# State-space phase of a two-layer encoder: input scaling, phase products and given states on VectorE, copied operands in a PSUM bank of their own

## Chip, cores, metric

One core of a Trainium2 chip runs the whole program. The metric is the device time of one execution in microseconds (us). Engines are named as in the profile: PE (TensorE matrix products, with PEld for its weight loads), DVE (VectorE), ACT (ScalarE), POOL (GpSimd), SP (SyncE, which issues most DMAs).

## The reference, cut to what matters

The program is one inference step of a two-layer encoder on 512 new positions of a prompt stream and 32 of a running stream, 1024 wide, in float32. Layer 0 mixes tokens with a complex diagonal state-space model (S5), layer 1 with retention; each is followed by cross-attention to memory tokens and a convolutional feed-forward part. The change lies in the S5 mixer alone:

```python
def s5_block(state, u, a_bar, b_bar, c):
    bu = jnp.einsum('gpc,blgc->blgp', b_bar, u.astype(jnp.complex64))
    bu = bu.at[:, 0].add(a_bar * state)
    a = jnp.broadcast_to(a_bar, bu.shape)
    _, xs = lax.associative_scan(_linear_combine, (a, bu), axis=1)
    y = jnp.real(jnp.einsum('gcp,blgp->blgc', c, xs))
    return xs[:, -1], y
```

There are 64 groups of 16 channels with 64 complex states each. `u` is the input after an RMS norm, so each position is scaled by one over its root mean square. The running stream starts from a given complex state, the prompt from zero. Beside the S5 mixer, both layers need keys and values of 256 memory tokens: four products of 256 x 1024 by 1024 x 1024, which do not depend on the stream.

## The kernel before, in words

**First phase, `phase1`.** It holds the S5 mixer of layer 0 up to its GELU, and, as filling, the memory keys and values of both layers. The 1024 channels go in eight tiles e = 0..7 of eight groups each. Time is cut in chunks of 8 positions, which gives 64 chunks for the prompt and 4 for the running stream, laid side by side in 70 columns (`POS`). The recurrence over chunks is turned into a real one: the states are multiplied by unit phases `ph` (parts `pr`, `pi`: 32 columns of states by 70 chunks), a real scan with the decay `rho8` runs along the chunks, and the result is turned back by the same phases.

The steps for one tile are functions of their own:

- `powers(e)` (V): scales the tile's input `u` by `ur`, one over the root mean square (L826, 128x560), and makes products of decay powers and input matrices: four on DVE (L834, L835), two sums on POOL (L836).
- `phases()` (P): once, makes `ph` by doubling. The squarings (L770 to L779) give columns 1, 2, 4, .., 64; five doublings fill the columns between by six complex products of 32, 96, 224, 480, 480 and 512 elements per partition. Each complex product is `cmul` (L580 to L589): six operations, of which the two second products (L585, L588) go to the engine `eng2`, here POOL, and four stay on DVE (L584, L586, L587, L589).
- `matrices(e)` (M): PE transposes (L848), ACT copies (L849, L855), PE products (L853, L856), a sum on DVE (L860) whose operand comes from POOL (L858), and eight small DMAs (L863).
- `states(e)` (S): PE products (L876) put the chunk inputs of a tile, real and imaginary, in two PSUM banks `v[0]`, `v[1]`. ACT copies a loaded operand `ca` (L880, two copies of 128x128) into free columns of the same two banks, and for five tiles also the input matrices of tile e+2 (`bbe`, L884, two copies of 128x64). DVE multiplies by the phases in place (L893 to L897). ACT then writes the given states into chunk column 65 of both banks (L898, L899).
- `carry(e)` (C): six products and sums on DVE from `ca` (L938 to L942).
- `scan(e)` (Z): on DVE, two scans (L915), the products back (L916, L917) and the sums (L921, L922); ACT copies the last states out (L924, L925).
- `outputs(e)` (O): PE products (L953, L954), GELU on ACT (L955), PE transposes (L963), ACT copies (L965, L966).

**Order.** The program text issues `PROLOGUE`: V0, P, M0, V1, S0, C0, Z0, M1, V2, and then for each e S(e+1), C(e+1), V(e+3), Z(e+1), O(e), M(e+2). At points marked F it puts in units of the memory keys and values: 16 units for layer 0 (plain products, L528) and 16 for layer 1 (weights split in two parts, products L240 to L242). A layer-1 unit's weights are loaded, cast and negated on ACT (L229, L230), and completed by an adding DMA issued from POOL (L235). Within the data's dependences each engine's queue is ordered by the framework's scheduler from a timeline that it estimates when the program is built; on the chip every engine goes through its queue in that order. An instruction that waits therefore holds up all that is behind it on its engine.

**Buffers.** The eight PSUM banks of this phase are one pool (`bank`). A tile taken from it is one whole bank and is free again after its last reader. The framework orders all accesses of different engines to one such tile, whichever columns they touch.

**After `phase1`** follow the GLU (`glu`, its weights split in L208 and L209 as everywhere after), attention, feed-forward, retention, and the second layer's attention and feed-forward, made of dense products on PE (L249).

Of the kernel before, what the change touches and what calls it, by code (L numbers as in the profile page):

```python
# [13 lines left out]
OP = mybir.AluOpType  # L14
# [3 lines left out]
P = 128  # L18
# [14 lines left out]
C = 16  # L33
NP = 32
L = 8
POS = 70
# [136 lines left out]
class Kernel:  # L173
# [417 lines left out]
    def phase1(self, sp):  # L591
        nc, io = self.nc, self.io
        V, A, PL = nc.vector, nc.scalar, nc.gpsimd
# [14 lines left out]
        def st(shape, tag, bufs=1, dt=F32):  # L608
            return sp.tile(shape, dt, tag=tag, bufs=bufs, name=self.name(tag))

        def load(key, shape, src=None, bufs=1, eng=None):
            t = st(shape, key, bufs)
            (eng or nc.sync).dma_start(out=t, in_=io[key] if src is None else src)
            return t
# [15 lines left out]
        s0 = load("s0", [P, 64])  # L630
# [15 lines left out]
        def sm(tag, keep=False):  # L646

            if keep:
                return st([P, N], tag)
            if not short:  # L650
                a = self.slot(5 * N)
                short.extend(a[:, n * N:(n + 1) * N] for n in range(5))
            return short.pop()
# [25 lines left out]
        k, r, q = (sm(f"q{n}") for n in range(3))  # L679
# [21 lines left out]
        for s in (1, 2, 4):  # L701
            o = [a[:, :, s + 1:2 * s + 1] for a in (Pr, Pi)]
            a = [a[:, :, 1:s + 1] for a in (Pr, Pi)]
            b = [a[:, :, s:s + 1].to_broadcast([P, N, s]) for a in (Pr, Pi)]
# [23 lines left out]
        V.tensor_tensor(out=u2, in0=am1, in1=li, op=OP.mult)  # L728
        V.tensor_tensor(out=ci_, in0=ci_, in1=u2, op=OP.subtract)
        V.tensor_tensor(out=ci_, in0=ci_, in1=den, op=OP.mult)  # L730
        bb = [st([P, NP, C], n) for n in ("bbr", "bbi")]
        bt = [self.slot(512).rearrange("p (n c) -> p n c", c=C) for _ in range(2)]
        for n in range(2):
            PL.tensor_tensor(out=braw[n], in0=braw[n], in1=gp, op=OP.mult)
# [13 lines left out]
        um, ut, ur = st([P, POS], "um"), st([P, POS], "ut"), st([P, POS], "ur")  # L748
# [4 lines left out]
        s0n = st([P, NP], "s0n")  # L753
# [11 lines left out]
        pr, pi = ph[:, 0], ph[:, 1]  # L765
        w1, w2, wt = (st([P, 2, NP, 1], f"w{n}") for n in range(3))

        def square(o, a):

            V.tensor_tensor(out=wt, in0=a, in1=a, op=OP.mult)  # L770
            V.tensor_tensor(out=o[:, 0], in0=wt[:, 0], in1=wt[:, 1], op=OP.subtract)
            V.scalar_tensor_tensor(out=o[:, 1], in0=a[:, 0], scalar=2.0, in1=a[:, 1], op0=OP.mult, op1=OP.mult)

        def unit(c):

            V.tensor_tensor(out=wt, in0=c, in1=c, op=OP.mult)
            V.tensor_tensor(out=wt[:, 0], in0=wt[:, 0], in1=wt[:, 1], op=OP.add)
            V.tensor_scalar(out=wt[:, 0], in0=wt[:, 0], scalar1=-0.5, scalar2=1.5, op0=OP.mult, op1=OP.add)
            V.tensor_tensor(out=c, in0=c, in1=wt[:, 0:1].to_broadcast([P, 2, NP, 1]), op=OP.mult)  # L779

        def phases():
            V.tensor_tensor(out=rho8, in0=rho[:, :NP], in1=rho[:, :NP], op=OP.mult)
            V.tensor_tensor(out=rho8, in0=rho8, in1=rho8, op=OP.mult)
            V.tensor_tensor(out=rho8, in0=rho8, in1=rho8, op=OP.mult)
            PL.memset(pr[:, :, 0:1], 1.0)
            PL.memset(pi[:, :, 0:1], 0.0)
            square(w1, csn[:, :, :NP].unsqueeze(3))
            square(w2, w1)
            square(ph[:, :, :, 1:2], w2)
            unit(ph[:, :, :, 1:2])  # L790
            s = 2
            while s <= 64:
                n = min(s, POS - 5 - s)
                square(ph[:, :, :, s:s + 1], ph[:, :, :, s // 2:s // 2 + 1])
                unit(ph[:, :, :, s:s + 1])
                if n > 1:
                    step = 16 if n == 32 else n
                    for o in range(0, n, step):
                        lo = max(o, 1)
                        w = o + step - lo  # L800
                        t = [self.slot(512)[:, :NP * w].rearrange("p (n s) -> p n s", s=w) for _ in range(2)]
                        self.cmul(V, [a[:, :, s + lo:s + o + step] for a in (pr, pi)],
                                  [a[:, :, lo:o + step] for a in (pr, pi)],
                                  [a[:, :, s:s + 1].to_broadcast([P, NP, w]) for a in (pr, pi)], t, PL)
                s *= 2
            for a in (pr, pi):
                PL.tensor_copy(out=a[:, :, 65:70], in_=a[:, :, 0:5])
# [9 lines left out]
        bbe = {e: [b3[:, n, e] for n in range(2)] for e in range(3)}  # L817
        self.g32 = []

        def powers(e):  # L820

            d = E[e]
            p0 = 4 * e
            d["cbd"] = load("cbd", [P, 2, 4, 2 * C], io["cbd"][e].rearrange("p (r n c) -> p r n c", r=2, n=4), 3)
            u = d["u"] = U[e].rearrange("p (g q) -> p g q", g=8)
            PL.tensor_tensor(out=u, in0=u, in1=ur.unsqueeze(1).to_broadcast([P, 8, POS]), op=OP.mult)  # L826

            sh = [P, 4, L, C]
            bs = [a.unsqueeze(2).to_broadcast(sh) for a in bbe.pop(e, [b[:, p0:p0 + 4] for b in bb])]
            pw = [a[:, p0:p0 + 4, :L].unsqueeze(3).to_broadcast(sh) for a in (Pr, PRn, PIn)]  # L830
            vb, vt = [self.slot(512).rearrange("p (n j c) -> p n j c", n=4, j=L) for _ in range(2)], \
                [self.slot(512).rearrange("p (n j c) -> p n j c", n=4, j=L) for _ in range(2)]
            for n in range(2):
                V.tensor_tensor(out=vb[n], in0=pw[n], in1=bs[n], op=OP.mult)  # L834
                V.tensor_tensor(out=vt[n], in0=pw[2], in1=bs[1 - n], op=OP.mult)  # L835
                PL.tensor_tensor(out=vb[n], in0=vb[n], in1=vt[n], op=OP.add)  # L836
            d["vb"] = [[b[:, i].rearrange("p j c -> p (j c)") for i in range(4)] for b in vb]
# [27 lines left out]
        def states(e):  # L865


            d = E[e]
            p0, g0 = 4 * e, 8 * e
            u, Vt = d["u"], d["Vt"]  # L870
            ca = load("ca", [P, 2, 8, C], io["ca"][e].rearrange("p (r n c) -> p r n c", r=2, n=8), 2)
            banks = [self.bank() for _ in range(2)]
            d["v"] = v = [b[:, :280].rearrange("p (n q) -> p n q", n=4) for b in banks]
            for n in range(2):
                for i in range(8):
                    nc.tensor.matmul(v[n][(i % 2) * 64:(i % 2 + 1) * 64, i // 2], lhsT=Vt[n][:, i * 64:(i + 1) * 64], rhs=u[:, i],  # L876
                                     start=True, stop=True)
            d["ca"] = [b[:, 280:408].rearrange("p (n c) -> p n c", c=C) for b in banks]
            for n in range(2):
                A.copy(d["ca"][n], ca[:, n])  # L880
            if e and e + 2 < KT:
                bbe[e + 2] = [b[:, 408:472].rearrange("p (n c) -> p n c", c=C) for b in banks]
                for n in range(2):
                    A.copy(bbe[e + 2][n], bb[n][:, p0 + 8:p0 + 12])  # L884
            phs = [a[:, p0:p0 + 4] for a in (pr, pi)]
            pos3 = [P, 4, POS]

            d0 = d["d0"] = st(pos3, "d0")
            PL.tensor_tensor(out=d0, in0=posmask.unsqueeze(1).to_broadcast(pos3),
                             in1=rho8[:, p0:p0 + 4].unsqueeze(2).to_broadcast(pos3), op=OP.mult)  # L890
            x = d["x"] = pair()
            for n in range(2):
                V.tensor_tensor(out=x[n], in0=v[n], in1=phs[0], op=OP.mult)  # L893
                V.tensor_tensor(out=v[n], in0=v[n], in1=phs[1], op=OP.mult)

            V.tensor_tensor(out=v[1], in0=x[0], in1=v[1], op=OP.subtract)
            V.tensor_tensor(out=v[0], in0=x[1], in1=v[0], op=OP.add)  # L897
            A.copy(v[1][:, :, 65], s0[:, p0:p0 + 4])  # L898
            A.copy(v[0][:, :, 65], s0n[:, p0:p0 + 4])  # L899

        def pair():
            t = self.slot(SLOT)
            return [t[:, n * 280:(n + 1) * 280].rearrange("p (n q) -> p n q", n=4) for n in range(2)]
# [41 lines left out]
        def outputs(e):  # L945
# [21 lines left out]
            self.g32.append(g32)  # L967

        fn = dict(V=powers, S=states, Z=scan, C=carry, M=matrices, O=outputs, P=lambda e: phases())
        done = set()  # L970

# [455 lines left out]
```

## Time and profile before

| | |
|---|---|
| three runs | 1888.02, 1890.13, 1890.9 us; median 1890.13 |
| the profiled execution | 1889.96 us, of which 1888.1 us are the profile's span |
| PE busy in the span | 1821.8 us (96%) |
| DVE, ACT, POOL busy | 1036.9, 636.5, 293.1 us |
| first dense product of the GLU (L249) | 243.04 us after the span's start |
| mean granted PE clock, 0 to 50, 50 to 100, 100 to 150, 150 to 200, 200 to 250 us | 0.97, 0.86, 0.84, 0.90, 0.93 |
| the same, 250 to 450 us | 1.00 |

The span is the time between the first and the last recorded instruction; the time of an execution has 1.9 us more. Times in rows count from the span's start. A row of a timeline gives start, duration, engine, line, operation, the tile written and the tiles read, the count of merged instructions, and in brackets the engine's idle time before it with what ended it. Where instructions of one line are merged, the duration is that of the whole row. A row of waits gives the total, the number of times and the longest.

### The profile page before, as it was taken

The page shows a single profiled execution, that of the slowest core. Times are in us where ns is not written, and L with a number is a line of the kernel's source. Part 1 is how long each engine was busy: PE and PEld are TensorE (multiplying, and loading weights), DVE is VectorE, ACT ScalarE, POOL GpSimd, SP SyncE. Part 2 cuts the span into 40 slices and gives each one's busy share as a digit, 9 for nine tenths or more (in the row PEclk, how much of TensorE's full clock was granted, in tenths as well). Part 3 has the DMA queues.
Part 4 walks back from the last instruction along what each step waited for, and adds up shares of the span by engine and source line. Part 5 has one row for each costly group of instructions (what it writes and reads, how often), then busy time and mean ns, then how long its engine had stood idle before and what let it go on. Part 6 is the DMA issues. An engine that isn't in the chain of part 4 may idle for free.

```text
span 1888.1 us, 32839 instructions
## 1 busy us (share of the span) xinstructions
PE 1821.8 (96%) x13815; PEld 1732.8 (92%) x13815; DVE 1036.9 (55%) x1827; ACT 636.5 (34%) x977; POOL 293.1 (16%) x368
## 2 busy tenths in 40 slices
PE   8877899999999999999999999999999999999998
PEld 7466799999999999999899899998899999999997
DVE  7686756545534535555545645546654554453553
ACT  3244554443323313333223222233443332232333
POOL 2522101011201202220000100100101121120221
PEclk9979999999999999999999999999999999999998
DMA  6737743122222222222222222222321222222221
GB/s 240 205 93 188 184 137 115 68 86 84 85 90 90 83 97 88 80 92 84 73 96 85 78 87 68 91 78 89 133 68 58 89 88 83 88 84 95 90 71 67
DMA packets 68274, 186.41 MB, mean 99 GB/s; under 512 B 9184, under 2 KB 18784, under 8 KB 68128
## 3 DMA queue, kind: packets, MB, share of 16 engines
q1 hardware_dynamic: 65536, 175.79, 28.0%
q0 software_dynamic: 2304, 8.39, 2.5%
q8 instruction: 108, 1.77, 0.4%
q14 instruction: 38, 0.31, 0.1%
q10 hardware_dynamic: 288, 0.15, 0.0%
HBM read 171.16 MB, written 10.77 MB: 96 GB/s over the span
## 4 chain that ended last, share of the span: by engine, by line
PE 84%; DVE 2%; ACT 1%; issue 1%; DMA 0%; ACTq 0%; DVEq 0%
PE ps L249 75%; PE ps L240 2%; PE ps L241 2%; PE ps L242 2%; PE ps L1351 1%; DVE wl L209 1%; PE ps L1340 0%; PE ps L1313 0%; PE ps L1073 0%; ACT wh L208 0%; PE ps L1287 0%; DMA wl<-in_w_v 0%; PE bank L1087 0%; DVE xl L308 0%; PE ps L345 0%
## 5 line engine op out<-in xcount | busy, mean ns | idle before, releaser
L249 PE MATMUL ps<-xh,wh 128*128 128x272 f32 x2432 | 507.5, 290 | 5.4 <-DVE x L372 3.6
L208 ACT CAST wh<-wr 128x1024 fp32r<-128x1024 f32 (+1 forms) x240 | 247.7, 1036 | 760.1 <-PE ps L249 641.2
L249 PE MATMUL ps<-xl,wh 128*128 128x272 f32 x2432 | 503.6, 288 | 0.0
L249 PE MATMUL ps<-xh,wl 128*128 128x272 f32 x2432 | 502.3, 288 | 0.0
L249 PE MATMUL ps<-r,wh 128*128 128x272 f32 x2688 | 449.0, 289 | 3.0 <-ACT r L966 1.6
L249 PEld LDWEIGHTS ps<-xh,wh 128*128 128x128 f32 x2432 | 380.6, 188 | 11.2 <-ACT r L314 3.8
L249 PEld LDWEIGHTS ps<-r,wh 128*128 128x128 f32 x2688 | 379.9, 189 | 6.4 <-ACT r L208 3.0
L249 PEld LDWEIGHTS ps<-xh,wl 128*128 128x128 f32 x2432 | 382.0, 188 | 2.3 <-issue 2.3
L249 PEld LDWEIGHTS ps<-xl,wh 128*128 128x128 f32 x2432 | 383.0, 189 | 0.3
L209 DVE TENSOR_TENSOR wl<-wr,wh 128x1024 fp32r<-128x1024 f32 (+1 forms) x240 | 296.8, 1239 | 98.0 <-ACT wh L208 89.2
L249 PE MATMUL ps<-r,wl 128*128 128x272 f32 x1344 | 278.1, 288 | 0.0
L249 PEld LDWEIGHTS ps<-r,wl 128*128 128x128 f32 x1344 | 211.1, 189 | 0.0
L372 DVE TENSOR_TENSOR x<-ps,x 128x544 f32<-128x544 f32 x96 | 69.3, 724 | 235.1 <-PE ps L249 234.9
L317 POOL TENSOR_TENSOR acc<-acc,r 128x544 f32<-128x544 f32 x36 | 58.7, 1631 | 466.1 <-ACT r L314 457.7
L1160 DVE TENSOR_TENSOR r<-ps,rr 128x544 f32<-128x544 f32 x44 | 31.9, 725 | 96.6 <-PE ps L249 96.6
L1150 DVE TENSOR_TENSOR r<-ps,rr 128x272 f32<-128x272 f32 x44 | 19.4, 442 | 117.7 <-PE ps L249 117.7
L208 ACT CAST r<-r 128x544 fp32r<-128x544 f32 x84 | 52.5, 650 | 65.4 <-POOL r L1161 25.7
L1153 POOL COPY nco<-r 128x2 f32<-128x2 f32 x44 | 13.9, 316 | 374.5 <-DVE r L1151 374.5
L1158 DVE SCALAR_TENSOR_TENSOR r<-r,conv,r 128x546 f32<-128x546 f32 x88 | 69.1, 785 | 3.5 <-ACT r L1156 1.9
L1161 POOL TENSOR_TENSOR r<-r,r 128x32 f32<-128x32 f32 x44 | 35.2, 799 | 206.2 <-ACT wh L208 186.2
L209 DVE TENSOR_TENSOR r<-r,r 128x544 fp32r<-128x544 f32 x84 | 59.3, 728 | 12.8 <-ACT r L208 12.6
L1211 POOL TENSOR_TENSOR r<-r,r 128x544 f32<-128x544 f32 x8 | 10.9, 1357 | 339.9 <-ACT wh L208 325.9
(347 smaller groups left out, 2036.4 us busy)
## 6 DMA issues: line engine op xcount, KB each, us to landing
wr<-in_w_r SPq DMA_DIRECT2D x48, 512.0 KB, 3.2
wr<-in_w_a SPq DMA_DIRECT2D x44, 512.0 KB, 3.2
wr<-in_w_g SPq DMA_DIRECT2D x44, 512.0 KB, 3.3
wr<-in_w_d SPq DMA_DIRECT2D x32, 448.0 KB, 3.4
wr<-in_w_k SPq DMA_DIRECT2D x16, 512.0 KB, 5.1
wr<-in_w_v SPq DMA_DIRECT2D x16, 512.0 KB, 3.6
wr<-in_w_q SPq DMA_DIRECT2D x16, 512.0 KB, 3.7
wr<-in_w_o SPq DMA_DIRECT2D x16, 512.0 KB, 3.3
```

The source lines that it names most:

```text
L208: self.nc.scalar.copy(hi, src)
L209: (self.nc.gpsimd if pool else self.nc.vector).tensor_tensor(out=lo, in0=src, in1=hi.bitcast(F32), op=OP.subtract)
L240: mm(out, lhsT=a[0], rhs=b[0], start=start, stop=False)
L241: mm(out, lhsT=a[0], rhs=b[1], start=False, stop=False)
L242: mm(out, lhsT=a[1], rhs=b[0], start=False, stop=stop)
L249: mm(ps[:, h, :TH], lhsT=ws[wi], rhs=x[xi][:, h * TH:(h + 1) * TH], start=start and n == 0, stop=stop and n == 2)
L317: add.tensor_tensor(out=self.acc, in0=self.acc, in1=sq, op=OP.add)
L372: self.nc.vector.tensor_tensor(out=self.halves(x), in0=src, in1=self.halves(x), op=OP.add)
L1150: V.tensor_tensor(out=ext[:, 2:2 + TH], in0=pa[:, 0, :TH], in1=r[:, :TH], op=OP.mult)
L1158: V.scalar_tensor_tensor(out=cv, in0=ext[:, t:t + W], scalar=cw[:, t, f:f + 1], in1=cv, op0=OP.mult, op1=OP.add)
L1160: V.tensor_tensor(out=self.halves(gr), in0=pg[:, :, :TH], in1=self.halves(r), op=OP.mult)
L1161: PL.tensor_tensor(out=gr[:, TP:], in0=gr[:, TP:], in1=cv[:, TP + 2:W], op=OP.mult)
```

## The change

Five edits in `phase1`, no other function is touched:

1. The input scaling L826 goes from POOL to DVE (eight instructions).
2. The second products of the six complex products in `phases` (L585, L588, twelve instructions) go from POOL to DVE.
3. The two writes of given states per tile (L898, L899, sixteen instructions) go from ACT to DVE.
4. `ca` and `bbe` are copied into a third bank `cb` that `states` takes from the pool, in place of free columns of the banks of `v`.
5. With one target bank, the two copies of `ca` become one, and so do the two of `bbe` (for this the two parts of `bb` are put in one tile `bball`).

```diff
-        bb = [st([P, NP, C], n) for n in ("bbr", "bbi")]
+        bball = st([P, 2, NP, C], "bb")
+        bb = [bball[:, n] for n in range(2)]
...
-                                  [a[:, :, s:s + 1].to_broadcast([P, NP, w]) for a in (pr, pi)], t, PL)
+                                  [a[:, :, s:s + 1].to_broadcast([P, NP, w]) for a in (pr, pi)], t)
...
-            PL.tensor_tensor(out=u, in0=u, in1=ur.unsqueeze(1).to_broadcast([P, 8, POS]), op=OP.mult)
+            V.tensor_tensor(out=u, in0=u, in1=ur.unsqueeze(1).to_broadcast([P, 8, POS]), op=OP.mult)
...
-            d["ca"] = [b[:, 280:408].rearrange("p (n c) -> p n c", c=C) for b in banks]
-            for n in range(2):
-                A.copy(d["ca"][n], ca[:, n])
+            cb = self.bank()
+            d["ca"] = [cb[:, n * 128:(n + 1) * 128].rearrange("p (n c) -> p n c", c=C) for n in range(2)]
+            A.copy(cb[:, :256].rearrange("p (r n c) -> p r n c", r=2, n=8), ca)
             if e and e + 2 < KT:
-                bbe[e + 2] = [b[:, 408:472].rearrange("p (n c) -> p n c", c=C) for b in banks]
-                for n in range(2):
-                    A.copy(bbe[e + 2][n], bb[n][:, p0 + 8:p0 + 12])
+                b4 = cb[:, 256:384].rearrange("p (n i c) -> p n i c", n=2, c=C)
+                bbe[e + 2] = [b4[:, n] for n in range(2)]
+                A.copy(b4, bball[:, :, p0 + 8:p0 + 12])
...
-            A.copy(v[1][:, :, 65], s0[:, p0:p0 + 4])
-            A.copy(v[0][:, :, 65], s0n[:, p0:p0 + 4])
+            V.tensor_copy(out=v[1][:, :, 65], in_=s0[:, p0:p0 + 4])
+            V.tensor_copy(out=v[0][:, :, 65], in_=s0n[:, p0:p0 + 4])
```

## The prediction

> **What bounds the kernel now.** I read the page first, then the chain that ended last, then the busy times by stage, then waits and timelines of single engines.
>
> ```profile
> span 1888.1 us, 32839 instructions
> PE 84%; DVE 2%; ACT 1%; issue 1%; DMA 0%; ACTq 0%; DVEq 0%
> ...
> 243.04 58.57 PE ps L249 x455
> ...
> 46.00:82.50 36.50, 35.76 (x148) 19.26 (x146) 20.43 (x34) 8.40 (x13) 21.32 (x24) 1.00 0.69 202
> 82.50:101.60 19.10, 6.29 (x58) 4.47 (x57) 18.82 (x34) 6.11 (x17) 7.01 (x7) 0.58 0.75 218
> 101.60:113.40 11.80, 6.58 (x33) 5.96 (x33) 11.71 (x26) 4.87 (x12) 2.88 (x3) 0.64 0.13 34
> 113.40:180.50 67.10, 57.01 (x561) 50.77 (x561) 50.33 (x106) 32.55 (x76) 19.71 (x22) 0.93 0.59 144
> 180.50:243.00 62.50, 48.03 (x360) 39.60 (x358) 38.12 (x77) 30.52 (x70) 9.42 (x11) 0.92 0.68 169
> ```
>
> The chain is PE for 84% of the span, and from 243.04 us on it is dense products in long unbroken pieces. The change touches nothing behind that point, so its worth is the time by which 243.04 moves. The lower rows are the stretch before it: length, then busy time of PE, PEld, DVE, ACT and POOL, granted clock, DMA share, GB/s. Up to 82.5 us PE is full (35.76 of 36.50). Between 82.5 and 113.4 it is busy 12.87 of 30.9 us, at a clock of 0.58 and 0.64, while DVE is full. So 18.0 us of PE time lie open there; at full clock the 12.87 would be 6.29 x 0.58 + 6.58 x 0.64 = 7.9, another 5.0. After 113.4 PE is idle 10.1 us in 67.1 and 14.5 us in 62.5: a loop over tiles that neither engine fills.
>
> Why DVE is full but late is in the timelines of POOL and DVE.
>
> ```profile
> 57.94 9.89 POOL L826 TENSOR_TENSOR u<-u,ur 128x560 f32<-128x560 f32 x8 [31.80 <-issue]
> 67.79 0.26 POOL L585 TENSOR_TENSOR r<-ph 128x32 f32<-128x32 f32 x1
> ...
> 68.28 2.49 POOL L836 TENSOR_TENSOR r<-r,r 128x512 f32<-128x512 f32 x2
> ...
> 85.45 1.23 POOL L588 TENSOR_TENSOR r<-ph 128x512 f32<-128x512 f32 x1
> ...
> 45.87 0.28 DVE L779 TENSOR_TENSOR ph<-ph,w 128x64 f32<-128x64 f32 x1
> ...
> 54.49 0.45 DVE L746 TENSOR_REDUCE ssum<-bank 128x70 f32<-128x280 f32 x1 [5.72 <-PE bank L744]
> ...
> 59.52 0.68 DVE L835 TENSOR_TENSOR r<-PIn,bank 128x512 f32<-128x512 f32 x1
> 68.08 0.30 DVE L586 TENSOR_TENSOR ph<-ph,r 128x32 f32<-128x32 f32 x1 [7.89 <-POOL r L585]
> ...
> 76.91 5.30 DVE L587 TENSOR_TENSOR ph<-ph 128x480 f32<-128x480 f32 x1
> ...
> 91.92 0.79 DVE L893 TENSOR_TENSOR r<-bank,ph 128x280 f32<-128x280 f32 x2
> ```
>
> POOL waits 31.8 us for the scale `ur`, then scales all eight inputs in a row (9.89 us); the first second product of the phases stands behind them at 67.79, although its inputs were there at 46.15 (L779, the last squaring step, ends then). DVE waits 7.89 us for it, goes on at POOL's pace, and reaches the first tile's L893 only at 91.92. The sums of V0 on POOL (L836), which PE's first transposes need, stand behind the scalings too.
>
> ```profile
> PE bank L848 <- POOL r L836: 7.2, 2, 6.7
> PE bank L876 <- ACT xl L849: 5.2, 3, 2.0
> PE bank L954 <- DVE r L922: 3.9, 2, 2.3
> PE bank L953 <- DVE r L921: 3.6, 1, 3.6
> PE bank L848 <- DVE xl L942: 2.0, 3, 0.8
> ...
> PE bank L241 <- DMA wl<-in_w_v: 6.6, 2, 5.1
> ```
>
> These are PE's waits between 46 and 243 us. The longest of the first four (6.7, 2.0, 2.3, 3.6) lie in the open stretch and together are 14.6 us: all four end with work that stands behind the phases on DVE, or behind POOL's backlog.
>
> **The change, part by part.** The durations for what moves to DVE:
>
> ```profile
> 36.08 0.22 DVE L584 TENSOR_TENSOR ph<-ph 128x32 f32<-128x32 f32 x1
> ...
> 71.86 0.39 DVE L589 TENSOR_TENSOR ph<-ph,r 128x96 f32<-128x96 f32 x1
> 72.16 0.38 DVE L584 TENSOR_TENSOR ph<-ph 128x224 f32<-128x224 f32 x1
> ...
> 74.89 0.66 DVE L584 TENSOR_TENSOR ph<-ph 128x480 f32<-128x480 f32 x1
> ...
> 83.26 0.68 DVE L584 TENSOR_TENSOR ph<-ph 128x512 f32<-128x512 f32 x1
> ...
> L372 DVE TENSOR_TENSOR x<-ps,x 128x544 f32<-128x544 f32 x96 | 69.3, 724 | 235.1 <-PE ps L249 234.9
> ...
> L898 ACT COPY bank<-s x8: 156/165/165, 94.3 to 226.4; 128x4 f32<-128x4 f32 x8
> ```
>
> *Phases (edit 2).* One operation of each of the six complex products costs 0.22 + 0.39 + 0.38 + 0.66 + 0.66 + 0.68 = 3.0 us together. The twelve moved ones are 6.0 us on DVE; all 36 are 18.0 us, and need nothing from another engine any more. Their inputs are complete at 46.15, and DVE's 5.72 us of idle time before L746 can take a part, so 12.3 us are left behind the scale. How many go there depends on the scheduler's estimate: the bounds are none and all.
>
> *Scaling (edit 1).* 724 ns for 544 elements gives 0.745 us for 560, eight times 6.0 us on DVE, against 9.89 on POOL. What goes: POOL is free for the sums of V0 as soon as L835 is done, at 60.2 instead of 68.28. On the path are the first scaling, which S0 needs, and at most the second; the other six fall behind or into DVE's waits (DVE is idle 16.8 us between 113.4 and 180.5), at no cost unless DVE becomes the pace.
>
> *The first L893.* V0 ends on DVE at 59.52 + 0.68 = 60.2. Add one scaling (0.75) and the 12.3 us of phases: 73.2. With V1 in between (four products of 0.68 and a scaling, 3.5) it is 76.7. So it comes 15 to 19 us earlier. If no idle time is used and V1 and all scalings go first: 60.2 + 6.0 + 18.0 + 2.7 = 86.9, 5 us earlier. If DVE is no limit at all, PE is: 18.0 + 5.0 = 23 us. PE is the nearer bound, because it has to do the layer-0 keys and values in any order. I take its four longest waits, 14.6, and half of what the clock can give, 2.5: 17 us. What is late next is PE itself.
>
> *The own bank (edits 4, 5).* One tile of the loop, and one exception:
>
> ```profile
> L893 DVE TENSOR_TENSOR r<-bank,ph 128x280 f32<-128x280 f32 x16 | 7.0, 441 | 9.2 <-ACT bank L884 8.8 <-ACT bank L880 0.4
> ...
> 137.36 0.21 ACT L924 COPY stout<-r 128x8 f32<-128x8 f32 x1 [4.68 <-DVE r L921]
> ...
> 141.47 1.19 PE L876 MATMUL bank<-u,xl 128*64 128x70 f32 x32
> ...
> 143.79 0.20 ACT L884 COPY bank<-bbr 128x64 f32<-128x64 f32 x1
> ...
> 144.03 0.45 DVE L893 TENSOR_TENSOR r<-bank,ph 128x280 f32<-128x280 f32 x1 [2.02 <-ACT bank L884]
> ...
> 132.31 1.22 PE L848 MATMUL bank<-ident,r 128*128 128x128 f32 x8 [0.59 <-DVE xl L942]
> ...
> 186.04 0.79 PE L241 MATMUL bank<-wl,r 128*128 128x512 f32 x1 [5.08 <-DMA wl<-in_w_v]
> ...
> 192.28 1.29 DVE L938 TENSOR_TENSOR xl<-bank,Pr 128x512 f32<-128x512 f32 x2 [7.21 <-ACT bank L899]
> ...
> 203.53 1.19 PE L876 MATMUL bank<-u,xl 128*64 128x70 f32 x32 [1.21 <-ACT xl L849]
> ```
>
> The bank is written by PE at 142.66 (141.47 + 1.19), but L893 starts at 144.03, 0.04 us after ACT's copy into the other columns ends. With a bank of its own the copy waits for the load alone, and L893 for PE: 1.37 of 2.02 us, a share of 0.68. The four such waits are 8.8 us with a longest of 3.6; in that one PE stalls behind it for a DMA (186.04), so I count 0.68 x (8.8 - 3.6) = 3.5 us on the loop's chain, which runs DVE, ACT, PE, ACT, DVE.
>
> [...]
>
> *Given states (edit 3).* No DVE row has four elements; the bounds are ACT's 0.165 us and DVE's 0.22 for 32. I take 0.2, two per tile, on the chain in the three tiles where a gain was counted: 1.2 us lost. In the sixth tile L938 waits 7.21 us for L899, which stands behind a cast on ACT that waits for PE. On DVE this goes; but PE is in arrears there, and its next tile waits only 1.21 us (203.53), so I count 1.2. The merged copies spare ACT time of which it has plenty: nothing.
>
> *Sum.* 17 + 3.5 - 1.2 + 1.2 = 20.5 us off the profiled execution's 1889.96 (0.17 below the runs' median): 1869.5 us.
>
> [...] DVE's L587 of 480 elements took 5.30 us at 76.91 while POOL ran its products, and 0.66 at 74.89. [...] An estimate from this page: V1's two sums, 2.49 us, block DVE once, which would make the sum 18.0 and the time 1872.
>
> **Rivals.**
>
> *The extra bank runs the pool dry (slower).* A tile of the loop takes ten banks and the keys' and values' own; now eleven, out of eight. That the pool is empty at times shows in L848's wait for L942, the last reader of a bank of `carry`. If the transposes must wait for the scan's end instead, they start at 137.36 and not at 132.31: 5.05 us for each of seven tiles, 35 us; 1869.5 + 35 = 1905. It decides from 20.5 / 7 = 2.9 us a tile on. Against it: L848's three waits are 2.0 us in all, and the copies leave no column of the `v` banks in use longer than before.
>
> *The front comes early, the weights do not.* The layer-1 units wait for an adding DMA; PE waited 6.6 us for it (5.1 at most). If a loop that starts 17 us earlier meets three such waits more, 15 us are lost: 1884.5. For it: the DMA share is 0.59 to 0.68 there. Against: those loads also follow the front.
>
> *The scheduler leaves DVE the same order.* Phases behind the scale, scalings first: 5 us at the front, less 1.2 for the states and one stall of DVE behind two sums of POOL (2.49, the L836 row; L587's 5.30 shows that such stalls occur): 1888.7. For it: L746 stands ahead of the phases in the queue today.
>
> *The tail goes too.* L938's 7.21 and PE's 5.08 were both the loop falling out of step once: 20.5 + 12.3, so 1857.
>
> **How the numbers follow.** A difference of 0.2% (3.8 us) is about what can be told from no change. Chances: the forecast 0.52, with its own range of 1860 to 1882 (front gain between 5 and 23, the states' cost between 0 and 2); empty pool 0.15; late weights 0.14; same order 0.11; tail too 0.08. Faster are the forecast, late weights and the tail: 0.74; same 0.11; slower 0.15. The predicted time is the forecast's, 1869.5. The range leaves out the empty pool and the ends of the tail and of "same order": 1850 to 1891.
>
> **What would show it.** Right: the phases run on DVE without a wait for POOL, and mostly before L746 or right behind V0; the first L893 is near 73 to 77; PE busy between 82.5 and 101.6 is over 12 us; L893 follows L876 directly; the first L249 of the GLU starts near 222. Wrong: if the scalings of later tiles stand ahead of the phases on DVE; if L848, L240 or L963 wait for a bank's last reader; if waits for `wl` grow by over 10 us; if the seven tiles after the first take longer than now.

## The result and the profile after

The changed kernel takes 1861.6 us (median of four runs, 1859.7 to 1864.6) against 1889.1 us for the kernel before in the same comparison: a ratio of 0.9857 [0.9838, 0.9875], 27.5 us less. The prediction was 1869.5 us, with a range of 1850 to 1891. The time lies inside the range, 7.9 us below the forecast. The range takes in the time of the kernel before as well, so lying inside it says little; that the kernel got faster is said by the interval. How the gain divides between the steps was foreseen wrongly. One of the nine executions of the run bbe_own below took 6860.6 us and is left out of its ratio.

The changed file has one line more ahead of the edits, so L893 of before is L894 of after, and so on for the lines of the S5 mixer. The first fence is from the page of the changed kernel, its span and the busy times; the second, from its chain that ended last in order of time, has the first dense product of the GLU.

```profile
span 1860.5 us, 32775 instructions
...
PE 1809.3 (97%) x13815; PEld 1723.5 (93%) x13815; DVE 1039.0 (56%) x1863; ACT 633.8 (34%) x948; POOL 275.3 (15%) x348
```

```profile
216.52 58.93 PE ps L249 x455
```

The GLU starts at 216.52 instead of 243.04 us: 26.5 of the 27.6 us by which the span is shorter. So the change was worth the move of that point, as the prediction took it.

Next the busy times by stage, up to the GLU, of the kernel before and then of the kernel after. Columns: window, length, busy us (and instructions) of PE, PEld, DVE, ACT and POOL, granted PE clock, DMA share, GB/s.

```profile
0.00:82.50 82.50, 76.22 (x323) 53.57 (x323) 55.35 (x183) 25.03 (x44) 34.19 (x49) 0.98 0.68 221
82.50:113.40 30.90, 12.86 (x91) 10.43 (x90) 30.53 (x59) 10.98 (x28) 9.89 (x10) 0.61 0.51 148
113.40:243.04 129.64, 105.05 (x918) 90.37 (x918) 88.48 (x183) 63.12 (x145) 29.12 (x33) 0.92 0.63 156
```

```profile
0.00:82.50 82.50, 74.15 (x323) 51.53 (x323) 65.66 (x218) 26.97 (x46) 18.47 (x33) 1.00 0.71 228
82.50:113.40 30.90, 17.86 (x139) 14.86 (x140) 26.66 (x59) 11.16 (x28) 10.03 (x11) 0.67 0.45 134
113.40:216.52 103.12, 91.07 (x871) 79.74 (x869) 83.26 (x186) 58.04 (x115) 26.22 (x31) 1.00 0.78 195
```

PE does the same products up to the GLU (1330 recorded rows in both). Its idle time in the three stages goes from 6.3, 18.0 and 24.6 us to 8.4, 13.0 and 12.1 us: 2.1 more, 5.0 less, 12.5 less. The products themselves take 183.1 us instead of 194.1, 11.0 less, at a granted clock that went from 0.92 to 1.00 in the loop. Together 26.4 us. So the open stretch from 82.5 to 113.4, where I expected most of the gain, gave 5.0 us of idle time, and the loop behind it 12.5.

A second way to divide the gain serves for all runs below: the start of the first tile's first phase product (L893, L894 after), the seven steps from there to the last tile's, and the rest to the GLU. Before: 91.92, then 131.9, then 19.2 us. After: 84.23, 117.2, 15.1. So 7.7 us came from the front, 14.7 from the loop, 4.1 from its end.

### The profile page after: what moved, and what is told of

The parts are those of the page before. It is cut to its first block, busy times and chain, and to the rows that moved or that the text cites. A ratio compares the mean times of both kernels' runs of the same rounds, so it can differ in the third digit from the quotient of the medians.

```text
span 1860.5 us, 32775 instructions
## 1 busy us (share of the span) xinstructions
PE 1809.3 (97%) x13815; PEld 1723.5 (93%) x13815; DVE 1039.0 (56%) x1863; ACT 633.8 (34%) x948; POOL 275.3 (15%) x348
## 4 chain that ended last, share of the span: by engine, by line
PE 85%; DVE 2%; ACT 1%; issue 1%; DMA 0%; ACTq 0%; DVEq 0%
PE ps L249 76%; PE ps L240 2%; PE ps L241 2%; PE ps L242 2%; PE ps L1352 1%; DVE wl L209 0%; PE ps L1341 0%; PE ps L1314 0%; PE ps L1074 0%; PE ps L1288 0%; ACT wh L208 0%; PE bank L1088 0%; DMA wl<-in_w_v 0%; DVE xl L308 0%; PE ps L345 0%
```

## Experiments

Two theories stood against each other. *Front*: the phases and scalings on DVE start the loop earlier, and the bank adds little. *Carry*: in the kernel before, a tile's carry (four products, which read `ca` in the banks of `v`, and two sums) depends on these banks; the framework orders a bank as a whole, so carry had to come behind the phase products of the same tile, on the chain DVE, ACT, PE that sets the step. With `ca` elsewhere it can be done earlier, while PE and ACT are still at the tile's inputs. A third theory, kept open because a new bank also means merged copies: the ACT copies themselves cost the time.

Beside the comparison of after, there are three groups of runs, each with its own runs of before (1889.5, 1889.0 and 1887.8 us). Times are medians; the three columns ahead of them are from one profiled execution of each kernel.

| kernel | edits | first L893 | seven steps | last to GLU | us | ratio to before |
|---|---|---|---|---|---|---|
| before | none | 91.9 | 131.9 | 19.2 | | 1 |
| after | 1 to 5 | 84.2 | 117.2 | 15.1 | 1861.6 | 0.9857 [0.9838, 0.9875] |
| bank_only | 4, 5 | 94.5 | 118.5 | 16.7 | 1877.4 | 0.9936 [0.9921, 0.9950] |
| engines_only | 1, 2, 3 | 82.0 | 136.0 | 18.6 | 1884.4 | 0.9973 [0.9962, 0.9984] |
| phases_only | 2 | 84.7 | 136.7 | 20.4 | 1888.4 | 0.9998 [0.9988, 1.0008] |
| phases_first | 1 to 5, phases issued first | 78.2 | 122.7 | 15.1 | 1862.2 | 0.9855 [0.9840, 0.9869] |
| bank_given | 3, 4, 5 | 95.3 | 121.4 | 17.1 | 1880.4 | 0.9945 [0.9925, 0.9965] |
| no_given | 1, 2, 4, 5 | 87.0 | 117.9 | 15.9 | 1865.6 | 0.9876 [0.9860, 0.9893] |
| bbe_own | only `bbe` in a bank of its own | 92.3 | 133.0 | 21.6 | 1894.3 | 1.0029 [1.0019, 1.0039] |
| ca_sbuf | `ca` read from SBUF, nothing else | 93.3 | 117.5 | 16.6 | 1870.8 | 0.9902 [0.9887, 0.9916] |
| bank_phases | 2, 4, 5 | 86.7 | 115.3 | 16.6 | 1867.6 | 0.9893 [0.9877, 0.9909] |
| bank_scal | 1, 4, 5 | 87.9 | 117.2 | 16.7 | 1865.6 | 0.9881 [0.9866, 0.9895] |
| all_sbuf | 1, 2, 3, no copies at all | 86.6 | 112.7 | 17.0 | 1860.1 | 0.9856 [0.9839, 0.9873] |
| mem_act | phases_first and another DMA queue | 77.8 | 122.6 | 15.2 | 1863.8 | 0.9866 [0.9852, 0.9881] |

The columns separate cleanly. The first L893 depends on edits 1 and 2: 77.8 to 87.9 us with either of them, 91.9 to 95.3 without. The seven steps depend on where `ca` is: 112.7 to 122.7 us where it is not in the banks of `v`, 131.9 to 136.7 where it is. The order in DVE's queue goes with it. In before, engines_only, phases_only and bbe_own, no tile has an operation of carry ahead of its first phase product; in ca_sbuf all eight tiles have all six ahead, in after seven of eight have four or more.

Six kernels ended outside the range of every theory written for them: bank_only, phases_only, bbe_own and ca_sbuf clearly, phases_first and no_given by less than 0.5 us.

### The change in two halves: bank_only and engines_only

bank_only has the kernel after's hunks on `cb` and `bball` alone:

```diff
+            cb = self.bank()
+            d["ca"] = [cb[:, n * 128:(n + 1) * 128].rearrange("p (n c) -> p n c", c=C) for n in range(2)]
+            A.copy(cb[:, :256].rearrange("p (r n c) -> p r n c", r=2, n=8), ca)
```

> Edits 4 and 5 alone: ca and bbe in a bank of their own, merged copies; scalings, phase products and given states stay where they were. Theory (the own bank frees carry's products from the banks of v, so DVE does them while PE and ACT prepare the next tile): the first L893 stays near 92 us, the steps from one tile's L893 to the next fall from 17 to 20 us to 15 to 16 us, the GLU starts 17 to 21 us earlier, time 1868 to 1872. Rival, the front (as predicted): the own bank is worth 3.5 us, time 1885. Rival, only both together: under 8 us, time 1881 or more.

engines_only has the other three (the second write of the given states is changed in the same way):

```diff
-                                  [a[:, :, s:s + 1].to_broadcast([P, NP, w]) for a in (pr, pi)], t, PL)
+                                  [a[:, :, s:s + 1].to_broadcast([P, NP, w]) for a in (pr, pi)], t)
-            PL.tensor_tensor(out=u, in0=u, in1=ur.unsqueeze(1).to_broadcast([P, 8, POS]), op=OP.mult)
+            V.tensor_tensor(out=u, in0=u, in1=ur.unsqueeze(1).to_broadcast([P, 8, POS]), op=OP.mult)
-            A.copy(v[1][:, :, 65], s0[:, p0:p0 + 4])
+            V.tensor_copy(out=v[1][:, :, 65], in_=s0[:, p0:p0 + 4])
```

> Edits 1, 2 and 3 alone: scalings, phase products and given states on DVE; ca and bbe stay in the banks of v. Theory: the first L893 comes near 84 us as in the changed kernel, the tiles after it keep steps of 17 to 20 us, time 1880 to 1885. Rival, the front: the 17 us are made here, time 1870 to 1873. Rival, only both together: 1884 or more.

The bank alone gave 12.2 us, the engines alone 5.1; together 27.5, so 10 us appear only with both. engines_only brings the first L893 forward by 9.9 us and loses 4.1 in the steps: of what the front won, the loop gave back a part. The waits of its phase products in the loop:

```profile
DVE r L893 <- ACT bank L880: 9.6, 1, 9.6
DVE r L893 <- ACT bank L884: 8.6, 4, 3.6
```

The wait of 7.21 us for the given states, which I had seen before, is gone, and a wait of 9.6 us for the copy of `ca` stands in its place. The four waits for L884 that I had priced at 3.5 us (8.8 in total before) are still there.

bank_only wins in the steps and starts the loop 2.6 us later than before. These are, before the GLU, PE's longest wait and then DVE's longest for ACT:

```profile
PE bank L849 <- POOL r L837: 11.7, 2, 11.1
```

```profile
DVE xl L939 <- ACT bank L881: 7.9, 2, 5.2
```

PE waits 11.1 us at a stretch for the sums of the second tile, V1. Its two waits for L837 (11.14 and 0.55 us) end at 91.79 and 93.46, as each of V1's two sums is done; none is for those of V0. The row of V1's sums on POOL:

```profile
90.47 2.93 POOL L837 TENSOR_TENSOR r<-r,r 128x512 f32<-128x512 f32 x2 [3.85 <-DVE r L836]
```

POOL itself waits there for V1's products on DVE. These stand behind phase operations that wait for POOL, and behind a carry product that is now put ahead in DVE's queue and waits 5.2 us for the copy of `ca`. In after PE's wait for these sums is 2.9 us.

Where do the 10 us lie that only both halves together bring? By the columns, not in the start of the loop: there the halves simply add (9.9 us earlier and 2.6 later, 7.7 earlier together). In the steps they do not: engines_only loses 4.1 us, bank_only wins 13.4, both win 14.7, which is 5.4 more than the sum. What the loop gives back to an early start, it no longer gives back when `ca` lies elsewhere.

### phases_only

Edit 2 alone, the first hunk of engines_only.

> Edit 2 alone: the twelve second products of the phases on DVE, the scalings stay on POOL. Theory: DVE no longer waits behind POOL's eight scalings; the first L893 is between 76 and 86 us, the loop is unchanged, 3 to 8 us faster, time 1881 to 1886. Rival, the front: 12 us or more, 1877 or less.

No gain, although the first L893 comes 7.2 us earlier: the steps take 4.8 us and the end 1.2 us more. An earlier start was worth nothing while the loop kept its pace.

### phases_first: the front as the prediction had it

The kernel after, with the phases issued ahead of V0, so that DVE takes them in its idle time before the root mean square:

```diff
-PROLOGUE = (("V", 0), ("P", 0), ("M", 0), ("V", 1),
+PROLOGUE = (("P", 0), ("V", 0), ("M", 0), ("V", 1),
```

> The changed kernel with one more edit: in the prologue the phases are put ahead of the first tile's powers, so that the queue of DVE has them before the scale of the input. Theory: DVE's idle 4.6 us before the input's sum of squares is filled and the first L894 comes at 72 to 78 us in place of 84, but the loop of the tiles and PE's keys and values set the end, so 0 to 6 us faster than the changed kernel, time 1855 to 1862. Rival, the front: the first L894's gain passes on in full, 8 to 12 us, time 1850 to 1854.

The first L894 starts at 78.15, 6.1 us earlier than in after, and the time is the same. PE's longest wait in the open stretch, and then the stretch itself in the busy times by stage:

```profile
PE bank L954 <- DMA M<-Fg: 7.9, 1, 7.9
```

```profile
82.50:113.40 30.90, 17.49 (x177) 15.62 (x176) 24.75 (x57) 12.53 (x29) 7.92 (x9) 0.74 0.60 165
```

PE is busy 17.49 us there, 17.86 in after. The wait for DVE is replaced by one for the DMAs that complete M0, which the output products of tile 0 need.

### mem_act: is it the layer-1 operands?

That wait would cost nothing if PE had other work at the head of its queue. The layer-1 units need the memory tokens' operands. So, in phases_first, the second load of the memory tokens was issued from ACT's queue instead of SP's (`eng` is SP for the first load and ACT for the second):

```diff
-                nc.sync.dma_start(out=m, in_=io["memT"][n // 2][:, (n % 2) * 512:(n % 2 + 1) * 512])
+                eng.dma_start(out=m, in_=io["memT"][n // 2][:, (n % 2) * 512:(n % 2 + 1) * 512])
```

> As phases_first (phases ahead of the first powers), and the second load of the memory tokens, which the layer-1 units need, is issued from the queue of ACT and not from SP, where it stands behind the first tile's eight small DMAs. Theory (a front that comes earlier brings nothing because PE has no layer-1 units to do there: their operands come at 94 us): the operands are there by 90 us, PE busy between 82.5 and 113.4 us rises from 17.5 to over 21 us, 3 to 7 us faster than phases_first, 1855 to 1859. Rival (PE's waits there are those of the tiles alone): 1861 to 1864.

The theory is not borne out, and not fully tested either. The operands' first scaling on ACT is at 92.4 us instead of 94.6, not by 90 as planned. PE's longest wait is 6.9 us, 7.9 in phases_first, and the time does not move. Three views of mem_act: the scaling of the operands with its first and last start, PE's longest wait in the open stretch, and the stretch itself.

```profile
L491 ACT ACTIVATE r<-r,gains x8: 491/498/508, 92.4 to 97.1; 128x256 fp32r<-128x256 f32 x8
```

```profile
PE bank L954 <- DMA M<-Fg: 6.9, 1, 6.9
```

```profile
82.50:113.40 30.90, 16.62 (x168) 14.40 (x161) 25.12 (x56) 12.20 (x28) 8.09 (x9) 0.79 0.57 161
```

A cause that remains possible is the order of PE's own queue (L954 stands ahead of the units); that was not tried.

### ca_sbuf and bbe_own: the carry or the copies

ca_sbuf is the kernel before, with one hunk: carry reads the loaded `ca` directly. No bank is added, and `bbe` stays in the banks of `v`.

```diff
-            d["ca"] = [b[:, 280:408].rearrange("p (n c) -> p n c", c=C) for b in banks]
-            for n in range(2):
-                A.copy(d["ca"][n], ca[:, n])
+            d["ca"] = [ca[:, n] for n in range(2)]
```

> ca is not copied to PSUM at all: carry reads it in SBUF where it was loaded; bbe stays in the banks of v, no bank is added. Theory: carry is free of the banks of v as with the own bank, so DVE does its products ahead of L893, steps of 15 to 18 us, time 1875 to 1882 (carry's products now have both inputs in SBUF and may meet POOL's). Rival, the extra bank or the merged copies are the gain: 1886 or more.

bbe_own is the opposite: `ca` stays in the banks of `v`, and `bbe` alone gets a bank and a merged copy (with `bball` as in the change). It takes away the very instruction, L884, on which L893 waited 8.8 us in the prediction's fence.

```diff
-                bbe[e + 2] = [b[:, 408:472].rearrange("p (n c) -> p n c", c=C) for b in banks]
-                for n in range(2):
-                    A.copy(bbe[e + 2][n], bb[n][:, p0 + 8:p0 + 12])
+                b4 = self.bank()[:, 256:384].rearrange("p (n i c) -> p n i c", n=2, c=C)
+                bbe[e + 2] = [b4[:, n] for n in range(2)]
+                A.copy(b4, bball[:, :, p0 + 8:p0 + 12])
```

> Only the input matrices bbe (L884) are copied into a bank of their own, in one copy for five tiles; ca stays in the banks of v. Theory (what counts is that the products of carry no longer depend on the banks of v): L893 waits for the copy of ca instead of that of bbe, the steps stay at 17 to 20 us, time 1884 to 1889. Rival, as predicted (the wait for L884 is the loop's loss): most of the own bank's gain, 1876 to 1880.

ca_sbuf is 18.2 us faster, bbe_own 5.3 us slower. First a row of bbe_own's waits of DVE in the loop, then, from ca_sbuf's timeline of DVE (its lines are numbered two lower: L936 is carry's first product and L891 the phase product), one tile:

```profile
DVE r L894 <- ACT bank L881: 7.7, 5, 4.8
```

```profile
137.03 0.90 DVE L919 TENSOR_TENSOR r<-r,bank 64x280 f32<-64x280 f32 x2
...
138.46 1.28 DVE L936 TENSOR_TENSOR xl<-ca,Pr 128x512 f32<-128x512 f32 x2
...
144.13 1.29 DVE L938 TENSOR_TENSOR bank<-ca,ait 128x512 f32<-128x512 f32 x2
145.34 0.68 DVE L940 TENSOR_TENSOR xl<-xl,bank 128x512 f32<-128x512 f32 x1
...
146.86 0.44 DVE L891 TENSOR_TENSOR r<-bank,ph 128x280 f32<-128x280 f32 x1
```

With L884 out of the way, the phase product waits for the copy of `ca` (L881 there) instead: 7.7 us in five waits, where 8.8 in four stood. A wait was renamed. Why bbe_own is slower than before is not shown; a part may be the bank more that it takes: behind 113.4 us PE's waits for banks that carry's sums read last (L942, there L943) are 5.9 us, against 3.0 in before. With `ca` free, carry's products stand ahead of the phase product of their tile. And although the copies of `bbe` stay in the banks in ca_sbuf, no phase product waits for them: the one wait left before L891 is for PE, 2.0 us. The third theory falls too: bbe_own has a merged copy of `bbe` and gains nothing, ca_sbuf merges none and drops only those of `ca`. How much of ca_sbuf's gain is the copies that it no longer makes is not separated in this run; but in bank_only the copies of `ca` are still made, and the steps are as short (118.5 and 117.5 us).

### all_sbuf: without the bank

The kernel after, with `ca` from SBUF and the copies of `ca` and `bbe` left out altogether (the same hunk as in ca_sbuf, on the kernel after, and no `cb`).

> Edits 1, 2 and 3 with no copies at all: carry reads ca, and the powers of the later tiles read their input matrices, in SBUF; neither the banks of v nor a bank of their own are used. Theory (the products of carry and the powers free of ACT and of the banks): no wait of L939 for ACT's copy (3.7 us in the changed kernel) and no bank taken, 0 to 6 us faster than the changed kernel, 1855 to 1862. Rival (two inputs in SBUF meet POOL's sums): DVE's products of powers take over 0.8 us in place of 0.68, 1863 to 1870.

1860.1 us: not to be told from after (0.9856 [0.9839, 0.9873] against 0.9857 [0.9838, 0.9875]). The rival's sign came in part: of the 29 products of powers that its timelines of DVE show, four took 1.75 to 1.78 us and the others 0.67 to 0.69, which did not show in the time. The bank of its own is not needed; that `ca` leaves the banks of `v` is. No run beat the changed kernel by more than the intervals.

### The given states: bank_given and no_given

```diff
-            A.copy(v[1][:, :, 65], s0[:, p0:p0 + 4])
-            A.copy(v[0][:, :, 65], s0n[:, p0:p0 + 4])
+            V.tensor_copy(out=v[1][:, :, 65], in_=s0[:, p0:p0 + 4])
+            V.tensor_copy(out=v[0][:, :, 65], in_=s0n[:, p0:p0 + 4])
```

bank_given adds this hunk to bank_only:

> Edits 3, 4 and 5: own bank and given states on DVE; scalings and phase products stay on POOL. Theory (the gain is made in the loop of the tiles by the own bank and the given states together, the front adds some 8 us): first L894 near 94 us, steps of 14 to 17 us between the tiles without one over 20, time 1868 to 1873. Rival, the given states do nothing: as the own bank alone, 1876 to 1879. Rival, the front is needed: 1876 or more.

no_given takes it out of the kernel after:

> Edits 1, 2, 4 and 5: the whole change without the given states, which stay on ACT behind its casts. Theory (given states and own bank take away the two waits of one place, so one without the other is worth less): one step of the loop over 20 us, time 1866 to 1872. Rival, the given states do nothing: 1860 to 1864.

Added to the bank the hunk makes the time 3.0 us longer, taken out of the whole change 4.0 us longer. In both pairs the intervals of the ratios overlap, so neither is clearly more than nothing. The first L893 and the steps both move by some us (95.3 and 121.4 against 94.5 and 118.5; 84.2 against 87.0). Which queue's order brings which us was not followed.

### Which of the front edits: bank_phases and bank_scal

Both are the kernel after with the given states on ACT; bank_phases also with the scaling on POOL, bank_scal also with the second phase products on POOL.

> Edits 2, 4 and 5: own bank and phase products on DVE; scalings on POOL, given states on ACT. Known so far: own bank alone 12 us faster, own bank with scalings and phase products 23. If the phase products bring the 11 between them (DVE and POOL no longer wait for each other in the front): 1865 to 1869. If the scalings bring them (POOL free for the sums of the first tiles): 1875 to 1879.

> Edits 1, 4 and 5: own bank and scalings on DVE; phase products on POOL, given states on ACT. If the scalings bring the 11 us: 1865 to 1869. If the phase products do: 1875 to 1879. If each takes away the wait that the other leaves, both kernels are at 1872 or more.

Either is enough. The kernels are from different groups, so the ratios to before are compared: with the bank, the phases bring 8.1 us, the scalings 10.4, both 11.3 (no_given). PE's wait of 11.1 us for V1's sums is gone in both kernels: its longest there is 1.0 us in bank_phases, and in bank_scal the transposes wait 5.1 us for DVE's L861 and not for POOL. The third expectation, that each takes away the wait that the other leaves, is out.

## Why the prediction was right, and where it was wrong

**The bound held, the sum was partly luck.** The tail behind the GLU's start gave 1.1 us, the stretch ahead of it 26.5. But of the two large terms one was too high and one too low: 17 us for the front, where edits 1 to 3 alone gave 5.1 us, and 3.5 us for the own bank, which alone gave 12.2. What both give together was not in the sum at all; counted on top of the bank, edits 1 to 3 bring 15 us.

**The front term, 17 us, was mis-sized.** It was to take PE's four longest waits, 14.6 us, out of the open stretch. PE's idle time there fell by 5.0 us. These are PE's longest waits there in after (82.5 to 113.4 us):

```profile
PE bank L955 <- DVE r L923: 5.7, 1, 5.7
PE bank L954 <- DMA M<-Fg: 3.4, 1, 3.4
PE bank L849 <- POOL r L837: 2.9, 1, 2.9
```

Three of the four are still there, 12.0 us in sum: the one for POOL fell from 6.7 to 2.9, the one for L922 (now L923) grew from 2.3 to 5.7, and where L953 waited 3.6 us for DVE it now waits 3.4 for a DMA. One reading behind the term was also wrong. The wait of 6.7 us is not for the sums of V0, which stand behind the scalings and end at 70.77, but for those of V1. In the kernel before:

```profile
87.95 2.90 POOL L836 TENSOR_TENSOR r<-r,r 128x512 f32<-128x512 f32 x2 [1.27 <-DVE r L835]
```

```profile
89.27 1.12 PE L848 MATMUL bank<-ident,r 128*128 128x128 f32 x4 [6.71 <-POOL r L836]
```

The first L893 was to come at 73 to 77 us and came at 84.23. The start of DVE's way there in after:

```profile
52.45 0.45 DVE L747 TENSOR_REDUCE ssum<-bank 128x70 f32<-128x280 f32 x1 [4.59 <-PE bank L745]
...
55.80 5.31 DVE L827 TENSOR_TENSOR u<-u,ur 128x560 f32<-128x560 f32 x8
61.02 0.68 DVE L835 TENSOR_TENSOR r<-Pr,bank 128x512 f32<-128x512 f32 x1
...
63.41 0.31 DVE L585 TENSOR_TENSOR r<-ph 128x32 f32<-128x32 f32 x1
63.65 1.30 DVE L588 TENSOR_TENSOR r<-ph 128x32 f32<-128x32 f32 x1
...
76.85 0.68 DVE L588 TENSOR_TENSOR r<-ph 128x512 f32<-128x512 f32 x1
...
79.84 0.68 DVE L939 TENSOR_TENSOR xl<-bank,Pr 128x512 f32<-128x512 f32 x1
...
82.43 0.68 DVE L589 TENSOR_TENSOR ph<-ph,r 128x512 f32<-128x512 f32 x1
...
84.23 0.80 DVE L894 TENSOR_TENSOR r<-bank,ph 128x280 f32<-128x280 f32 x2
```

Against the sum that led to 76.7: all eight scalings stand ahead of V0, so the phases begin 2.5 us later than counted (63.41, not 60.95). None of the 34 remaining phase operations lies in DVE's idle time before L747, which is still 4.59 us; they take 15.2 us, not 12.3. V1 takes 2.4 and not 3.5. Carry's products and a sum of M stand in between, 3.2 us that were not foreseen, because the own bank made them possible. That is 7.5 us. It was the sign named as wrong, scalings of later tiles ahead of the phases. But phases_first shows that the price of it was small: with the first L894 at 78.15, the 6.1 us were not turned into time. The failing step is "its four longest waits, 14.6": behind a wait that shrank stood another, for the DMAs of M0 (3.4 us in after, 7.9 in phases_first), and not work. PE's busy time from 82.5 to 101.6, expected over 12, is 8.13 us.

**The own bank, 3.5 us, was mis-sized by more.** bank_only gave 12.2, ca_sbuf 18.2. I had read the wait of L893 for L884 and priced it, where bbe_own shows that this wait, when L884 is taken away, moves to the copy of `ca`. What I did not read in the same timeline is the order behind it. From the kernel before, the tile whose row was quoted, and from after:

```profile
145.82 0.45 DVE L896 TENSOR_TENSOR bank<-r,bank 128x280 f32<-128x280 f32 x1
146.17 1.28 DVE L938 TENSOR_TENSOR xl<-bank,Pr 128x512 f32<-128x512 f32 x2
...
147.97 1.29 DVE L940 TENSOR_TENSOR bank<-bank,ait 128x512 f32<-128x512 f32 x2
...
150.96 1.28 DVE L942 TENSOR_TENSOR xl<-xl,bank 128x512 f32<-128x512 f32 x2
152.15 1.36 DVE L915 TENSOR_TENSOR_SCAN bank<-d,bank 128x280 f32<-128x280 f32 x2
```

```profile
131.43 0.42 DVE L550 TENSOR_TENSOR acc<-bank,mr 128x256 f32<-128x256 f32 x1 [1.00 <-PE bank L242]
131.77 0.68 DVE L939 TENSOR_TENSOR xl<-bank,Pr 128x512 f32<-128x512 f32 x1
...
133.56 0.69 DVE L941 TENSOR_TENSOR bank<-bank,ait 128x512 f32<-128x512 f32 x1
134.16 0.44 DVE L894 TENSOR_TENSOR r<-bank,ph 128x280 f32<-128x280 f32 x1
```

Before, carry's six products and sums (3.85 us) are all behind the tile's phase products: they start only when L893 to L897 have started, and the scan, with the steps that hang on it, follows them. In after, four of the six are done between 131.77 and 134.16. PE writes the tile's banks in that time (L877 at 131.32, 1.20 us, followed by the output products of the tile before), so these 2.4 us are work that DVE would otherwise do later on the chain. The steps got shorter by 14.7 / 7 = 2.1 us.

The sign "L893 follows L876 directly" is half right: DVE's waits for L884 are gone, but the gap behind the products is filled with carry. The waits of L894 and L939 in the loop are now these two, one time each:

```profile
DVE r L894 <- PE bank L877: 7.0, 1, 7.0
DVE xl L939 <- ACT bank L881: 3.7, 1, 3.7
```

**The clock, 2.5 us, was mis-sized.** I counted half of what it could give in the open stretch alone. There it hardly rose (0.61 to 0.67); the gain is in the loop, where I had counted none, and 11.0 us over the whole front. That it is the clock shows in busy time times granted clock up to the GLU, which stayed: 194.1 x 0.90 = 175 us before, 183.1 x 0.95 = 174 after. PE's output products in the loop of the kernel before, once at a granted clock of 0.50 (162 to 163 us) and, under 3 us later, at 1.00 (165 to 166):

```profile
162.39 0.63 PE L953 MATMUL bank<-M,u 128*69 128x128 f32 x2
162.82 0.64 PE L954 MATMUL bank<-xl,r 128*69 128x128 f32 x2
...
165.20 0.38 PE L954 MATMUL bank<-xl,r 128*69 128x128 f32 x2
165.42 0.38 PE L953 MATMUL bank<-M,u 128*69 128x128 f32 x2
```

Pairs of the same products follow each other at 0.43 us and then at 0.22. In these two kernels, from 82.5 us on, the clock is lower where PE is idle for a larger share: 0.61 where it is idle 18.0 of 30.9 us, 0.67 with 13.0 of 30.9, 0.92 with 24.6 of 129.6, 1.00 with 12.1 of 103.1. If the one brings the other, shorter idle times in the loop paid twice. That is my reading of these four stages and not shown: no run varied the idle time alone, and in the open stretch engines_only had 0.59 with 14.0 us idle, phases_only 0.68 with 18.8.

**The given states, 0 us in sum, were not told from nothing:** 3.0 us lost with the bank alone, 4.0 won in the whole change, both within overlapping intervals. DVE's copies cost less than the 0.2 us I took: 0.15 and 0.17 us in after.

```profile
124.61 0.15 DVE L900 COPY bank<-s0n 128x4 f32<-128x4 f32 x1
...
125.17 0.17 DVE L899 COPY bank<-s 128x4 f32<-128x4 f32 x1
```

**The estimate against the change: about 1 us, not 2.5.** In after one of the moved operations is long beside POOL's sums: L588 of 32 elements takes 1.30 us (quoted above), 1.0 more than L585 of the same size, and ends at 64.95, when these sums end (64.88):

```profile
62.38 2.50 POOL L837 TENSOR_TENSOR r<-r,r 128x512 f32<-128x512 f32 x2 [37.34 <-DVE r L836]
```

The second of V0's sums starts at 63.6 and takes 1.27 us, so L588, from 63.65 on, lasts as long as that sum. In the kernel before, L587 of 480 elements took 0.65 us at 75.77, with no operation of POOL beside it, and 5.30 us at 76.91, while POOL ran its four products of that size (77.32 to 81.67); the prediction's 0.66 us at 74.89 is a row of L584. What the two engines share there no run shows. I had counted both sums of V1 in full; beside these (82.33 to 85.47) no operation of DVE was longer than its like (the products of 512 elements 0.68 to 0.69 us), and the first of the sums took 1.91 us in place of 1.27.

**The rivals.** *Empty pool*: in after no wait of PE's transposes, keys or values for a bank's last reader is longer than 1.3 us (L240 for L550), and all_sbuf, without the eleventh bank, takes the same time. bank_phases has waits of PE for a bank that carry reads (L941), 3.9 and 3.0 us in the front, and bbe_own the 5.9 us named above, so the mechanism exists, but not in after. *Late weights*: PE's waits for `wl` fell from 6.6 to 3.2 us. *Same order*: half true, the scalings do stand first; but its sum had nothing for the own bank, and 27.5 us came off where it gave 1.3. *The tail goes too*, 1857 us, came nearest by its number (4.6 us off; the forecast 7.9) and not by its reason: the 7.21 us wait went, but in engines_only, where it went too, a wait of 9.6 us took its place.

**What stays open.** In bank_only a carry product stands ahead of phase operations and costs a wait of 5.2 us for ACT's copies; with either front edit there is none or 0.2 us of it (bank_phases, bank_scal), and why was not tested. That the steps are shorter because carry is done while PE writes the banks is read from the order of the queues and from the sizes (2.4 and 2.1 us), not tried by an order of its own. The few us that the given states bring or cost, and PE's wait for M0's DMAs in a front that starts early, are not explained further than above.

## What to carry to other kernels

Where an operand of one step lies in free columns of a buffer that another step writes, ask which steps it puts in order: the cost is not the copy's wait that the profile names, but what could have been done earlier and now stands behind. Test a wait's worth by taking away only what ends it: twice here (L884, L899) another wait took its place and the steps did not get shorter. Bringing the start of a loop forward is worth only as much as the loop's own step can use; phases alone gave 7.2 us at the front and nothing at the end, but 8 us of time on top of the own bank.

## What the runs showed of the hardware beyond that

With 12.5 us less of idle time in the loop, PE's granted clock there went from 0.92 to 1.00, and the same number of products up to the GLU took 11.0 us less. In after's DVE timeline the durations of operations in a row overlap: the twelve phase operations of 480 elements (68.22 to 74.48, two of them below) last 0.65 us each and start 0.56 to 0.57 us apart, so the sum of these durations is some 14% too long; the prediction's 18.0 us for the phases is a sum of that kind.

```profile
70.50 0.65 DVE L585 TENSOR_TENSOR r<-ph 128x480 f32<-128x480 f32 x1
71.06 0.65 DVE L588 TENSOR_TENSOR r<-ph 128x480 f32<-128x480 f32 x1
```
